# A retention layer's products in another order: rotary sums on VectorE, the second values' products behind the queries, the last head by halves of the tokens

## The chip, the cores and the metric

The kernel runs on one core of a Trainium2 chip. The metric is the device time of one launch in microseconds, the median of several runs. TensorE (PE) multiplies matrices and writes to PSUM; VectorE (DVE) and ScalarE (ACT) work on PSUM and SBUF; GpSimd (POOL) works on SBUF; SyncE (SP) issues the DMAs of this stage. Each engine takes its instructions in the order of its own queue, and semaphores order the engines among each other.

## The reference

Two layers of a diffusion backbone over 512 latent tokens with 256 context tokens and 1024 features, in fp32. The change touches layer 1, a bidirectional retention mixer with four heads (query and key width 256, value width 512), and the first steps of its feed-forward layer. Cut to what matters:

```python
q_x, k_x, v_x, g_x = split(h_x @ w_qkvg)          # 4 heads: 256, 256, 512, 512 each
q_x, k_x = rope_2d(q_x), rope_2d(k_x) * k_scale   # [x1 cos - x2 sin, x1 sin + x2 cos]
k_c, v_c = split(h_c @ w_qkvg[:, k and v])        # context: keys and values alone
state_f = retention_final_state(k_c, v_c); state_b = ...
o = retention_chunked(q_x, k_x, v_x, state_f) + flip(retention_chunked(flipped, state_b))
y = (o - mean) * rsqrt(var + EPS) * gn_gain       # per head, over its 512 values
x = x + mx[2] * ((silu(g_x) * y) @ w_o)
x = x + mx[5] * swiglu(modulate(rms_norm(x), mx[3], mx[4]))
```

## The kernel before, in words

Tiles have 128 partitions. Features lie on partitions, tokens along the free dimension, except in values, gates and the heads' outputs, where tokens lie on partitions. Every fp32 product is made of three matmuls on a high and a low part of each operand: `split` (line 163) casts a tile to its high part on ACT and subtracts it on VectorE for the low part (L164 and L165 in the profile). Weights come as 512 KB chunks of a stream in DRAM, through two raw buffers `wraw` (four others, `wx`, serve single chunks), each loaded by one DMA on SP's queue. Their two parts take one of four pairs of buffers in turn (`w_parts`, line 125); a pair is free when the product that read it has ended.

The retention layer multiplies the 512 tokens by the weights of one head at a time. In a head, query and key weights, and gate and value weights, are multiplied together as blocks: tokens are taken in halves (`HALVES`, line 31) and features in halves, and seven products of quarter size stand for eight. `quarter_of` names their operands: "11", "12" and "22" are quarters of the normed input, 1 to 4 are sums of quarters that `token_sums` (line 1125) makes once, in head 0. `product_q` and `product_v` (lines 1167, 1178) issue the matmuls of one such product: 24 of 256 columns for queries and keys, 24 of 512 for values and gates.

A head's loop body (line 1244) runs, in program order:

1. the first values' product into the two banks Z (`values_first`, issued in the head before, for head 0 ahead of the loop; line 1229);
2. the second values' product into banks X, and the context's values into the banks pj (lines 1252 to 1265);
3. keys into Y, X and pj (1271 to 1286), then the combined weights of the queries and five products (1289 to 1311);
4. the rotary of the queries (`rope_pair`, line 1191: two products on VectorE, L1196 and L1197, their sum or difference on GpSimd, L1198, and a split);
5. the combined weights of gates and values (1315 to 1328), the rotary of the keys, and products 2, 3 and "22" into the Z banks, which ACT copies out (L1333, L1336, L1340);
6. for each of six key tiles the scores, their decay factors and the sums over values (`scores`, `accumulate`, line 1347);
7. two more gate products into Z (1384 to 1397), the norm of the head's output, the gates, and the next head's first values;
8. 16 transposes of the gated output, the next head's context values, and eight output tiles added to the residual `xr` (`out_tile`, line 1442).

The last head makes its output tiles for the first half of the tokens and then for the second (line 1470). While the second half runs, the first half is normed for the feed-forward layer, whose first weights are split in between (`first_weights`, line 1462); its first products run on the first half too (`first_two`, line 1521), with the second half's norm (`second_half`) behind them.

The order on each engine is not written out by hand in this layer. The planner of the tile framework walks through the program, favours what comes earlier in it, and takes an instruction when, by its cost model, its operands and buffers are ready; `after` (line 91) adds an order between two instructions without a wait of its own. A tag's buffer count limits how far ahead a tile can be taken: 2 banks each for X, Y, Z and pj, 2 for `hn` and `sq`, 8 for `qk`.

Of the kernel before, what the change touches and what calls it, by code (L numbers as in the profile page):

```python
# [14 lines left out]
P = 128  # L15
# [34 lines left out]
def dit_kernel(ctx, tc, xT, cT, crow, small, consts, masks, tabs0, tabs1, jtab, adaQ, adaN, adaT, wst, out):  # L50
# [49 lines left out]
    def lnexp(*args, **kw):  # L100
        ins = nc.scalar.activation(*args, **kw)  # L101
        after(ins, [turn["pre"]])
        turn["lnexp"].append(ins)

# [1004 lines left out]
    def split_chunk(raw):  # L1109
        w = w_parts(qp)  # L1110
        split(raw, *w)
        return w

# [11 lines left out]
    def token_sums(hm, part, sh2, sums, behind=()):  # L1125
# [4 lines left out]
        for k in range(4):  # L1130
# [5 lines left out]
            for i, t in enumerate((t2, t1)):  # L1136
                split(t, *sums[2 * k + i])
# [8 lines left out]
    def latent_norm():  # L1146
        hm, b, y = [t_qk(F32) for _ in range(KT)], mods[1, 0], ssq[0]
        for k, t in enumerate(hm):
            nc.vector.scalar_tensor_tensor(t, xr[k], acol[1, 0, 0][:, k:k + 1], y, mult, mult)
# [4 lines left out]
        return hm  # L1154
# [36 lines left out]
    def rope_pair(o, cos1, sin1):  # L1191

        res = []
        for op, f0, f1 in ((sub, cos1, sin1), (add, sin1, cos1)):
# [3 lines left out]
            nc.gpsimd.tensor_tensor(a, a, b, op=op)  # L1198
# [5 lines left out]
    def strips(hd):  # L1204
# [6 lines left out]
        lnexp(dx[:, 512:896], jt[:, 128:512], AF.Exp, scale=lf)  # L1211
# [17 lines left out]
    def values_first(hd):  # L1229

        w = [split_chunk(chunk(chunk_base + 16 * hd + 4 + i)) for i in range(2)]
# [3 lines left out]
        return w, Y, ins  # L1235
# [6 lines left out]
    hm = latent_norm()  # L1242
    ahead_v = values_first(0)
    for hd in range(RH):
        bq = chunk_base + 16 * hd
        bv, bg = bq + 4, bq + 8


        b11, Yv, ins = ahead_v
        if hd == 0:  # L1250
            normed = context_norm([ins])
        b21 = [split_chunk(chunk(bv + i)) for i in (2, 3)]
        vt = [T(rp, 512, "res", 12) for _ in range(4)]
        for t in range(2):
            nc.scalar.copy(vt[t], Yv[t])
        Xv = [W4("X"), W4("X")]
        product_v(Xv, quarter_of("12"), b21, True)
        for t in range(2):
            nc.vector.tensor_tensor(vt[t], vt[t], Xv[t], op=add)
        if hd == 0:  # L1260
            cv = context_values(b11)
        product_v(cv, context_half(1), b21, False)
        vt += [T(rp, 512, "y0", 1), T(qp, 512, "vc", 1)]
        for t in range(2):
            nc.scalar.copy(vt[4 + t], cv[t])
# [483 lines left out]
```

## Time and profile before

| what | us |
|---|---|
| median of 3 runs | 1814.02 (1813.11 to 1815.79) |
| the profiled execution | 1812.0 |
| its span, first to last instruction | 1810.2 |
| TensorE busy in it | 1732.1 |
| VectorE busy | 1352.0 |
| retention layer, about | 905 to 1453 of the span |

The page of the profile gives shares over the whole span. Its views by window, by engine in order of time, and by wait are what the prediction works with. In a row of the timeline stand the start, the length, the engine, the line, the operation, the tiles written and read, the shape and the count; square brackets give the idle time before it and what ended it. In a row of windows stand the stretch, its length, and for each engine its busy time and number of instructions, then the granted TensorE clock (PEclk, 1.00 is full), the share of the DMA engines and GB/s.

### The profile page before, as it was taken

The page shows a single profiled execution, that of the slowest core. Times are in us where ns is not written, and L with a number is a line of the kernel's source. Part 1 is how long each engine was busy: PE and PEld are TensorE (multiplying, and loading weights), DVE is VectorE, ACT ScalarE, POOL GpSimd, SP SyncE. Part 2 cuts the span into 40 slices and gives each one's busy share as a digit, 9 for nine tenths or more (in the row PEclk, how much of TensorE's full clock was granted, in tenths as well). Part 3 has the DMA queues.
Part 4 walks back from the last instruction along what each step waited for, and adds up shares of the span by engine and source line. Part 5 has one row for each costly group of instructions (what it writes and reads, how often), then busy time and mean ns, then how long its engine had stood idle before and what let it go on. Part 6 is the DMA issues. An engine that isn't in the chain of part 4 may idle for free.

```text
span 1810.2 us, 27644 instructions
## 1 busy us (share of the span) xinstructions
PE 1732.1 (96%) x10876; PEld 1538.7 (85%) x10876; DVE 1352.0 (75%) x2327; ACT 835.0 (46%) x1461; POOL 163.9 (9%) x291
## 2 busy tenths in 40 slices
PE   6899999999999999999988999998999999999999
PEld 4777776799999999999877887887897889999998
DVE  6697786786688877777688758758757788777774
ACT  5476676363423333333454524524534454445432
POOL 0035334000000000000001001001001010000000
PEclk9999999999999999999988999999999999999999
DMA  9510002542244534343333424433433223233222
GB/s 338 224 36 24 24 2 82 182 141 86 90 134 126 162 118 143 118 147 117 95 107 128 156 89 130 146 94 129 146 113 97 93 71 98 90 117 117 84 92 82
DMA packets 59891, 206.69 MB, mean 114 GB/s; under 512 B 6640, under 2 KB 7024, under 8 KB 59504
## 3 DMA queue, kind: packets, MB, share of 16 engines
q1 hardware_dynamic: 52848, 179.75, 30.8%
q0 software_dynamic: 6912, 25.17, 4.6%
q8 instruction: 85, 1.39, 0.3%
q14 instruction: 46, 0.38, 0.1%
HBM read 202.80 MB, written 2.10 MB: 113 GB/s over the span
## 4 chain that ended last, share of the span: by engine, by line
PE 69%; DVE 16%; DMA 6%; ACT 4%; issue 3%; POOL 2%; SPq 0%; DVEq 0%; ACTq 0%; POOLq 0%
PE Y L834 12%; PE Z L834 6%; PE pj L148 6%; PE pj L149 6%; PE pj L147 6%; PE Z L1187 5%; PE X L834 3%; DVE wlo L165 3%; DMA wraw<-in_wst_dram 3%; PE pT L706 2%; DVE y L270 2%; DMA adaw<-in_adaT_dram 2%; PE pO L718 2%; PE S L683 2%; PE pj L1187 2%
## 5 line engine op out<-in xcount | busy, mean ns | idle before, releaser
L164 ACT CAST whi<-wraw 128x1024 fp32r<-128x1024 f32 x173 | 181.1, 1050 | 288.5 <-PE Z L149 73.6
L165 DVE TENSOR_TENSOR wlo<-wraw,whi 128x1024 fp32r<-128x1024 f32 x173 | 210.7, 1222 | 47.6 <-ACT whi L164 47.4
L834 PE MATMUL Y<-aq,whi 128*128 128x384 f32 x576 | 156.0, 335 | 0.6 <-ACT hn L974 0.5
L140 DVE TENSOR_TENSOR wlo<-wraw,whi 128x1024 fp32r<-128x1024 f32 x84 | 103.5, 1232 | 40.0 <-ACT whi L139 39.4
L252 DVE SCALAR_TENSOR_TENSOR res<-pj,mod,res 128x512 f32<-128x512 f32 (+1 forms) x112 | 81.5, 729 | 65.0 <-PE pj L149 63.9
L139 ACT CAST whi<-wraw 128x1024 fp32r<-128x1024 f32 x84 | 88.1, 1050 | 89.9 <-DMA wraw<-in_wst_dram 28.0
L834 PEld LDWEIGHTS Y<-aq,whi 128*128 128x128 f32 x576 | 104.8, 188 | 1.5 <-ACT hn L974 0.9
L834 PE MATMUL Y<-aq,wlo 128*128 128x384 f32 x288 | 96.6, 335 | 1.6 <-DVE wlo L165 1.6
L1187 PE MATMUL Z<-whi,sA 128*128 128x512 f32 x256 | 83.9, 400 | 6.6 <-ACT whi L164 3.6
L101 ACT ACTIVATE pr<-pr,stat,qs 128x513 f32<-128x513 f32 (+2 forms) x96 | 74.2, 776 | 30.7 <-DVE stat L690 29.9
L697 POOL TENSOR_SCALAR pr<-pr,stat 128x512 f32<-128x512 f32 (+2 forms) x96 | 67.1, 713 | 86.6 <-DVE stat L694 66.4
L270 DVE CUSTOM_DVE_ANT_0 y<-adaw,crow,small_sb 128x1024 bf16<-128x1024 f32 x48 | 61.4, 1278 | 14.5 <-DMA adaw<-in_adaT_dram 14.4
L1198 POOL TENSOR_TENSOR hn<-hn,sq 128x512 f32<-128x512 f32 x16 | 30.1, 1886 | 436.2 <-DVE sq L1197 432.6
L147 PE MATMUL pj<-ax,whi 128*128 128x512 f32 x176 | 68.7, 390 | 0.8 <-DVE res L252 0.8
L149 PE MATMUL pj<-ax,whi 128*128 128x512 f32 x176 | 68.7, 390 | 0.0
L148 PE MATMUL pj<-ax,wlo 128*128 128x512 f32 x176 | 68.5, 389 | 0.0
L706 PE MATMUL pT<-const_sb,pr 128*128 128x128 f32 x352 | 58.1, 284 | 9.8 <-POOL pr L697 7.6
L147 PE MATMUL pj<-act,whi 128*128 128x512 f32 x168 | 66.0, 393 | 0.0
L148 PE MATMUL pj<-act,wlo 128*128 128x512 f32 x168 | 65.9, 392 | 0.0
L1187 PEld LDWEIGHTS Z<-whi,sA 128*128 128x128 f32 x256 | 49.1, 192 | 19.6 <-ACT gate L1333 5.6
L149 PE MATMUL pj<-act,whi 128*128 128x512 f32 x168 | 65.5, 390 | 0.0
L706 PEld LDWEIGHTS pT<-const_sb,pr 128*128 128x128 f32 x352 | 38.8, 141 | 30.3 <-POOL pr L697 18.3
(504 smaller groups left out, 5382.1 us busy)
## 6 DMA issues: line engine op xcount, KB each, us to landing
wraw<-in_wst_dram SPq DMA_DIRECT2D x238, 512.0 KB, 3.6
adaw<-in_adaT_dram POOLq DMA_DIRECT2D x32, 512.0 KB, 3.9
wx<-in_wst_dram SPq DMA_DIRECT2D x24, 512.0 KB, 4.5
adan<-in_adaQ_dram SPq DMA_DIRECT2D x16, 512.0 KB, 8.2
adan<-in_adaN_dram SPq DMA_DIRECT2D x16, 512.0 KB, 8.7
crow<-in_adaT_dram POOLq DMA_DIRECT2D x16, 512.0 KB, 4.2
res<-in_xT_dram SPq DMA_DIRECT2D x16, 256.0 KB, 5.8
adaw<-in_adaT_dram SPq DMA_DIRECT2D x8, 512.0 KB, 4.1
```

The costliest lines, as they stand in the source:

```text
L139: nc.scalar.copy(hi, raw)
L140: nc.vector.tensor_tensor(lo, raw, hi, op=sub)
L147: nc.tensor.matmul(o, whi, xhi, start=first, stop=False)
L148: nc.tensor.matmul(o, wlo, xhi, start=False, stop=False)
L149: return nc.tensor.matmul(o, whi, xlo, start=False, stop=last)
L164: nc.scalar.copy(hi, t)
L165: return nc.vector.tensor_tensor(lo, t, hi, op=sub)
L252: return nc.vector.scalar_tensor_tensor(res[d], o, mods[l, s][:, part, d:d + 1], res[d], mult, add)
L270: after(nc.vector.tensor_tensor_reduce(junk, w, cr[:, s * 1024:(s + 1) * 1024], 1.0, sm_t[:, C_ADAB + l * 48 + j:C_ADAB + l * 48 + j + 1], ...
L706: nc.tensor.transpose(tp[:, a * P:(a + 1) * P], self.pr[(0, 2, 1, 3)[a]][:, ki * P:(ki + 1) * P], ident)
L834: nc.tensor.matmul(o, p, r, start=first and k + i == 0, stop=k == 3 and i == 2, skip_group_check=not first)
L1187: ins = nc.tensor.matmul(o, p, r, start=first and k + i == 0, stop=k == 3 and i == 2, skip_group_check=not first)
```

## The change

It touches the following.

- `rope_pair`: the sum of the two rotary products goes from GpSimd to VectorE.
- `latent_norm`: called for tiles 0 to 3 and 4 to 7, with the split of the first values' weights (`first_weights_v`) between them in program order, and the later tiles put behind that split on VectorE. The first values are copied out of Z in `values_first` itself.
- `other_values`: the second values' product and the context's values (step 2) become a function, called ahead of the keys in head 0 and behind the queries' rotary in heads 1 to 3. The context's keys `kc` go to a bank X instead of pj.
- `strips(0)`: its exponentials stand behind the token sums.
- The second half of the last gate product (tile 1) comes behind the gating of tiles 2 and 3, and in the last head also behind the transposes and casts of the second half of the tokens.
- The last head's output tiles run for the second half of the tokens first, in banks pj and Z, with the transposes and casts of the first half behind the fourth tile; then for the first half in X and Y. The norm of the feed-forward layer begins with the second half; an output tile's residual stands behind the norm four tiles back, and two of its four first weights behind the sixth norm. `first_two` begins with the second half.

```diff
-    def add_square(s, k, t, c=slice(None), eng=nc.vector, tmp=t_sq):
+    def add_square(s, k, t, c=slice(None), eng=nc.vector, tmp=t_sq, fresh=True):
...
-            if c.start in (None, 0):
+            if fresh:
...
-    def latent_norm():
-        hm, b, y = [t_qk(F32) for _ in range(KT)], mods[1, 0], ssq[0]
-        for k, t in enumerate(hm):
-            nc.vector.scalar_tensor_tensor(t, xr[k], acol[1, 0, 0][:, k:k + 1], y, mult, mult)
+    def latent_norm(ks, behind=()):
+        b, y = mods[1, 0], ssq[0]
+        for k in ks:
+            hm.append(t_qk(F32))
+            t = hm[k]
+            after(nc.vector.scalar_tensor_tensor(t, xr[k], acol[1, 0, 0][:, k:k + 1], y, mult, mult), behind)
...
-            nc.gpsimd.tensor_tensor(a, a, b, op=op)
+            nc.vector.tensor_tensor(a, a, b, op=op)
...
-    def strips(hd):
+    def strips(hd, behind=()):
...
-        lnexp(dx[:, 512:896], jt[:, 128:512], AF.Exp, scale=lf)
+        after(lnexp(dx[:, 512:896], jt[:, 128:512], AF.Exp, scale=lf), behind)
...
-    def values_first(hd):
-
-        w = [split_chunk(chunk(chunk_base + 16 * hd + 4 + i)) for i in range(2)]
+    def first_weights_v(hd):
+        return [split_chunk(chunk(chunk_base + 16 * hd + 4 + i)) for i in range(2)]
+
+    def values_first(w):
+
         Y = [W4("Z"), W4("Z")]
         ins = product_v(Y, quarter_of("11"), w, True, (0,))
         product_v(Y, quarter_of("11"), w, True, (1,))
-        return w, Y, ins
+        vt = [T(rp, 512, "res", 12) for _ in range(4)]
+        for t in range(2):
+            nc.scalar.copy(vt[t], Y[t])
+        return w, Y, vt, ins
...
-    hm = latent_norm()
-    ahead_v = values_first(0)
+    latent_norm(range(4))
+    b11 = first_weights_v(0)
+    latent_norm(range(4, KT), [last_split[0]])
+    b11, Yv, vt, ins = values_first(b11)
+    normed = context_norm([ins])
     for hd in range(RH):
...
+        def other_values():
+
+            b21 = [split_chunk(chunk(bv + i)) for i in (2, 3)]
+            Xv = [W4("X"), W4("X")]
+            product_v(Xv, quarter_of("12"), b21, True)
+            for t in range(2):
+                nc.vector.tensor_tensor(vt[t], vt[t], Xv[t], op=add)
+            c = cv if hd else context_values(b11)
+            product_v(c, context_half(1), b21, False)
+            vt.extend((T(rp, 512, "y0", 1), T(qp, 512, "vc", 1)))
+            for t in range(2):
+                nc.scalar.copy(vt[4 + t], c[t])
+
         if hd == 0:
...
+            other_values()
         k11, k21 = split_chunk(chunk(bq)), split_chunk(chunk(bq + 1))
         if hd == 0:
-            token_sums(hm, 0, T(qp, 64, "sh2", 1), h_sum, [normed])
-            dx, dcx = strips(0)
+            sums = token_sums(hm, 0, T(qp, 64, "sh2", 1), h_sum, [normed])
+            dx, dcx = strips(0, [sums])
         cos1, sin1 = rope_tables()
-        Y, X, kc = W4("Y"), W4("X"), pj()
+        Y, X, kc = W4("Y"), W4("X"), W4("X")
...
         qh = rope_pair(qt, cos1, sin1)
+        if hd:
+            other_values()
...
-        product_v(Zg, quarter_of(4), w22, False)
-        for t in range(2):
-            nc.vector.tensor_tensor(gate[t], gate[t], Zg[t], op=add)
+        product_v(Zg, quarter_of(4), w22, False, (0,))
...
+        gated(2)
+        gated(3)
+        if last:
+            transposes(1)
+            turned(HALVES[1])
+        product_v(Zg, quarter_of(4), w22, False, (1,))
+        for t in range(2):
+            nc.vector.tensor_tensor(gate[t], gate[t], Zg[t], op=add)
+            gated(t)
+        if not last:
+
+            b11, Yv, vt, ins = values_first(first_weights_v(hd + 1))
+            transposes(1)
+            transposes(0)
+            turned(slice(0, SX))
+            cv = context_values(b11)
...
-        for i, c in enumerate(HALVES):
+        for i, c in ((0, HALVES[1]), (1, HALVES[0])):
             for d in range(KT):
-                ins = out_tile(d, c)
-                add_square(0, d, xr[d], c, eng=(nc.vector, nc.gpsimd)[i])
+                ins = out_tile(d, c, "XY" if i else "jZ")
+                add_square(0, d, xr[d], c, eng=(nc.vector, nc.gpsimd)[i], fresh=i == 0)
+                if (i, d) == (0, 3):
+                    transposes(0)
+                    turned(HALVES[0])
                 if (i, d) in ((0, 5), (0, 7)):
                     first_weights(wx_parts)
-                if (i, d) in ((1, 3), (1, 5)):
-                    first_weights(hW_parts)
...
+                if (i, d) == (1, 1):
+                    rms(0, HALVES[1])
                 if i == 1 and d > 1:
-                    modulate(1, 0, 1, d - 2, xr, hx[d - 2], HALVES[0], hm[d - 2][:, HALVES[0]], [ins])
-        for k in (KT - 2, KT - 1):
-            modulate(1, 0, 1, k, xr, hx[k], HALVES[0], hm[k][:, HALVES[0]])
+                    done.append(second_norm(d - 2, HALVES[1], [ins]))
+                if i == 1 and d > 3:
+                    after(ins, done[d - 4:d - 3])
+        done += [second_norm(k, HALVES[1]) for k in (KT - 2, KT - 1)]
+        for _ in range(2):
+            first_weights(hW_parts, done[5:6])
...
-        for i, c in enumerate(HALVES):
+        for i in (1, 0):
+            c = HALVES[i]
             for f, (go, uo) in enumerate(banks):
-                project_pair(ahead[2 * f:2 * f + 2], half(i), (go[:, c], uo[:, c]), None if i + f else second_half, 5)
+                project_pair(ahead[2 * f:2 * f + 2], half(i), (go[:, c], uo[:, c]), second_half if i > f else None, 5)
```

New functions: `transposes(i)` issues the eight transposes of tiles 2i and 2i + 1 into banks X and Y; `turned(c)` scales and splits them for the tokens `c` (ACT and VectorE, L1434 and L1435 before); `gated(n)` is the silu of a gate tile and its product with the normed output; `second_norm` calls `modulate` for one tile and half.

More of the change, by code (lines that the diff above doesn't have):

```diff
@@ L1136, in token_sums @@
             for i, t in enumerate((t2, t1)):
-                split(t, *sums[2 * k + i])
+                last = split(t, *sums[2 * k + i])
+        return last
     def first_quarters(k, half):
@@ new lines, in dit_kernel @@
+        gated(2)
[7 more added lines that the diff above has]
+            gated(t)
+        if not last:
+            b11, Yv, vt, ins = values_first(first_weights_v(hd + 1))
[3 more added lines that the diff above has]
+            cv = context_values(b11)
@@ L1459, in dit_kernel, with first_weights @@
                       for n in ("hM", "hW", "hX"))
-        ahead, hx, hm = [], [], []
-        def first_weights(room):
+        ahead = []
+        def first_weights(room, behind=()):
             raw = w_raw()
-            ahead.append(room())
-            split(raw, *ahead[-1])
+            hi, lo = room()
+            ahead.append((hi, lo))
+            after(nc.scalar.copy(hi, raw), behind)
+            nc.vector.tensor_tensor(lo, raw, hi, op=sub)
         wx_parts = lambda: (T(qw, 1024, "wx", 4, F32R), T(qw, 1024, "wx", 4, F32R))
```

76 lines of the change are left out of this document (30 added, 46 removed).

## The prediction

> **What bounds the kernel now.** The page comes first: which engine is busy, and which engine the chain that ended last runs through.
>
> ```profile
> span 1810.2 us, 27644 instructions
> PE 1732.1 (96%) x10876; PEld 1538.7 (85%) x10876; DVE 1352.0 (75%) x2327; ACT 835.0 (46%) x1461; POOL 163.9 (9%) x291
> PE 69%; DVE 16%; DMA 6%; ACT 4%; issue 3%; POOL 2%; SPq 0%; DVEq 0%; ACTq 0%; POOLq 0%
> ```
>
> TensorE is the bound. The change removes no matmul, so it can only win time in which TensorE stands or runs slow. Such time is found by windows: the length of a stretch, less its matmuls times their undisturbed step. The first two rows give the steps, the next seven the stretches of the retention layer (905 to 1490 us) in which TensorE stands longest.
>
> ```profile
> core 0: us, PE busy (x) PEld busy (x) DVE busy (x) ACT busy (x) POOL busy (x), PEclk, DMA share, GB/s
> 1019.87:1030.75 10.88, 10.88 (x50) 9.01 (x48) 9.93 (x21) 5.56 (x8) 0.00 (x0) 1.00 0.51 205
> 1087.56:1099.08 11.52, 11.52 (x98) 11.47 (x96) 8.92 (x11) 6.15 (x11) 0.00 (x0) 1.00 0.68 216
> 907.97:929.45 21.48, 14.58 (x53) 10.88 (x52) 16.44 (x28) 10.54 (x19) 2.00 (x2) 0.76 0.51 171
> 951.73:988.50 36.77, 30.55 (x172) 26.39 (x170) 33.49 (x36) 16.98 (x26) 5.35 (x4) 0.86 0.35 112
> 1098.96:1122.39 23.43, 19.36 (x87) 15.22 (x86) 20.38 (x25) 10.33 (x16) 7.71 (x4) 0.93 0.24 78
> 1228.68:1253.05 24.37, 19.28 (x88) 15.17 (x87) 21.32 (x26) 10.54 (x16) 7.71 (x4) 0.93 0.26 83
> 1359.35:1382.37 23.02, 19.12 (x88) 15.21 (x86) 19.98 (x23) 10.04 (x16) 7.71 (x4) 0.93 0.19 53
> 1420.46:1452.97 32.51, 29.01 (x211) 27.72 (x209) 20.67 (x38) 15.62 (x28) 3.85 (x6) 0.90 0.35 117
> 1452.97:1485.13 32.16, 27.93 (x196) 26.15 (x195) 28.30 (x58) 19.78 (x35) 2.33 (x5) 0.89 0.32 100
> ```
>
> 48 matmuls of 512 columns in 10.88 us are 0.227 us each, 96 of 256 columns in 11.52 us are 0.12. By the code (missing records don't matter) and these steps:
>
> - **head 0, start** (907.97): 48 of 512, three small ones: 11.2 of 21.48 us, **10.3 lost**.
> - **head 0, queries to scores** (951.73): 121 of 256, 48 of 512: 25.4 of 36.77, **11.4 lost**.
> - **heads 1 to 3, the same place**: 25 of 256, 60 of 512: 16.6 us; lost **6.8, 7.8 and 6.4**, together 21.0.
> - **last head's output** (1420.46): 16 transposes (1.7 us), 192 of 256, two small: 25.0 of 32.51, **7.5 lost**.
> - **start of the feed-forward layer** (1452.97): 192 of 256, two small: 23.3 of 32.16, **8.9 lost**.
>
> Together 59.1 us. More than this the change cannot win.
>
> Why TensorE stops in heads 1 to 3 is read from the timelines of four engines in head 1:
>
> ```profile
> 1117.95 0.50 PE L1187 MATMUL Z<-whi,aq 128*128 128x512 f32 x1 [2.88 <-ACT gate L1336]
> 1119.56 1.05 PE L1187 MATMUL Z<-whi,aq 128*128 128x512 f32 x2
> 1120.41 0.63 PE L1187 MATMUL Z<-wlo,aq 128*128 128x512 f32 x1
> 1116.79 0.62 ACT L164 CAST qk<-hn 128x512 fp32r<-128x512 f32 x1 [4.79 <-POOL hn L1198]
> 1117.32 0.58 ACT L1336 COPY gate<-Z 128x512 f32<-128x512 f32 x1
> 1113.97 4.01 POOL L1198 TENSOR_TENSOR hn<-hn,sq 128x512 f32<-128x512 f32 x2 [7.04 <-DVE sq L1197]
> 1101.66 0.68 DVE L1197 TENSOR_TENSOR sq<-gate,rj 128x512 f32<-128x512 f32 x1
> 1102.87 1.78 DVE L1197 TENSOR_TENSOR sq<-gate,rj 128x512 f32<-128x512 f32 x1
> ```
>
> TensorE needs bank Z, which ACT must copy out (L1336). That copy stands in ACT's queue behind the cast of the rotated keys, and the cast waits 4.79 us for POOL's rotary add. The wait costs more than its length: from 1119.56 to 1120.41 two matmuls take 0.85 us, 0.43 each. That lasts some 9 matmuls, about 1.8 us more. The Trainium skill's page "TensorE: Matmul & The Clock Gate" (section "Why this matters for your kernels") puts the half clock behind gaps of about 3 us and more; here one of 2.88 us sufficed. By that rule a wait of 1 to 2 us left over in the changed kernel would cost its own length alone, as in the sum below.
>
> Head 0 is another case, VectorE's:
>
> ```profile
> 917.69 1.21 DVE L165 TENSOR_TENSOR wlo<-wraw,whi 128x1024 fp32r<-128x1024 f32 x1
> 917.16 0.80 PE L1187 MATMUL Z<-wlo,aq 128*128 128x512 f32 x1 [4.00 <-DVE wlo L165]
> 920.69 1.05 ACT L164 CAST whi<-wraw 128x1024 fp32r<-128x1024 f32 x1 [4.14 <-DMA wraw<-in_wst_dram]
> 976.34 1.22 PE L1187 MATMUL Z<-whi,sA 128*128 128x512 f32 x2 [3.55 <-ACT whi L164]
> 905.00:990.00 85.00, 71.77 (x393) 61.79 (x394) 76.46 (x114) 43.96 (x76) 10.37 (x8) 0.88 0.35 113
> ```
>
> The first values' products wait 4.00 us for the low part of their weights (L165), which VectorE makes only after the norm of all eight tiles; the next weights' DMA waits for the same buffer (4.14 us). But VectorE is busy 76.46 of 85 us: here it is the second bound.
>
> **The change part by part.** The profiled execution took 1812.0 us (span 1810.2); the median of the runs is 1814.02, so I add 2.0 at the end.
>
> *Rotary adds from POOL to VectorE* (L1198, four a head). Head 1's rows for what VectorE does beside them:
>
> ```profile
> L165 DVE TENSOR_TENSOR qk<-hn,qk 128x512 fp32r<-128x512 f32 x4 | 4.2, 1060 | 1.9 <-ACT qk L164 1.8
> L1197 DVE TENSOR_TENSOR sq<-gate,rj 128x512 f32<-128x512 f32 x4 | 3.8, 952 | 0.0
> ```
>
> Added: 16 VectorE adds of L1197's shape, 0.68 us undisturbed, 2.7 us a head. Gone: POOL's, the 4.01 us pair above included, and the stretching of VectorE's work beside them: 4 x (1.06 + 0.95 - 2 x 0.68) = 2.6 us a head. So VectorE's load stays level, and the path from product to cast shortens by 1 to 2 us at each add. POOL's queue issues no DMA here and loses nothing that others wait for.
>
> *X and context products behind the queries* (heads 1 to 3). 24 matmuls into X and 24 into pj, 48 x 0.227 = 10.9 us, go from before the keys to between the queries and product 2. They are cover: now 13.6 us of Z products (60 of 512) lie between the queries' end and the first score, then 24.5. What has to be done under them:
>
> ```profile
> 1040.00:1080.00 40.00, 40.00 (x194) 33.79 (x192) 21.41 (x24) 10.58 (x14) 0.00 (x0) 1.00 0.31 91
> 1065.17:1122.39 57.22, 53.15 (x325) 47.14 (x324) 42.22 (x47) 22.29 (x34) 7.71 (x4) 0.97 0.32 97
> L165 DVE TENSOR_TENSOR wlo<-wraw,whi 128x1024 fp32r<-128x1024 f32 x173 | 210.7, 1222 | 47.6 <-ACT whi L164 47.4
> L164 ACT CAST whi<-wraw 128x1024 fp32r<-128x1024 f32 x173 | 181.1, 1050 | 288.5 <-PE Z L149 73.6
> wraw<-in_wst_dram SPq DMA_DIRECT2D x238, 512.0 KB, 3.6
> ```
>
> From the end of the output tiles to the first score VectorE works 42.2 us; after, 42.2 + 2.7 - 2.6 = 42.3 us against 50.4 us of matmuls (57.22 less 6.8): it fits, at 84%. The order is tighter than the sum. w_parts (line 125) turns four pairs of buffers, and a pair is free when its product ends. With the second values' weights (two pairs) behind the queries, those of product 3 can be cut only when the context product ends: 1.05 (ACT) + 2 x 1.22 (VectorE) = 3.5 us, under the 5.4 us of product 2. Those of the last values follow under product 3, likewise. In SP's queue their two loads now stand behind the queries' and ahead of the gate's. The later one needs a buffer that is free when the last query weights are cut, some 17 us after the keys begin (keys 96 and queries 120 of 256: 25.9 us); it lands 3.6 us after issue, is cut by 23 and needed at 27. The gate's loads behind it make product 2's weights ready at about 31, needed at 36.8. Queued behind the rotated queries' casts on ACT are copies of X, pj and Z; the casts now wait for VectorE alone. The keys lose their cover of 10.9 us, but their weights can be cut during the output tiles, when VectorE is half idle (21.41 of 40 us). The bounds for the three heads are 21.0 (all stalls go) and, if VectorE comes late for both pairs, 6; I take **16** (5 us left), near the upper end because of the 84%.
>
> *Head 0*: its second values stay ahead of the keys. The split of the first weights goes between the norm of tiles 0 to 3 (all that the first product reads) and 4 to 7. The 4.00 us wait and the 4.14 us DMA wait mostly go. But the gain then stops at VectorE: it has 8.5 us of idleness in the 85, and the adds leave its load level. Bounds 2 and 8.5; I take **7**. The strips' six exponentials are put behind the token sums. ACT, busy 43.96 of 85 us, hides them; uncovered they are at most 6 x 0.91 = 5.5 us by the longest of them in a later head:
>
> ```profile
> 1145.62 0.91 ACT L101 ACTIVATE dcx<-rj,dcol,lg 128x640 f32<-128x640 f32 x1
> ```
>
> *Last head by halves*. Now: transposes wait for all gates, then the output for the casts of all four tiles.
>
> ```profile
> 1425.79 0.44 PE L147 MATMUL X<-qk,whi 128*128 128x256 f32 x1 [2.01 <-DVE qk L1435]
> 1454.55 0.38 PE L147 MATMUL X<-hx,wx 128*128 128x256 f32 x1 [1.43 <-ACT hx L241]
> 1454.12 1.22 DVE L165 TENSOR_TENSOR wlo<-wraw,whi 128x1024 fp32r<-128x1024 f32 x1 [0.25 <-ACT whi L164]
> 1455.26 0.48 DVE L242 SCALAR_TENSOR_TENSOR hx<-hm,mod,hx 128x256 fp32r<-128x256 f32 x1
> 1472.80 0.39 PE L147 MATMUL X<-hx,wx 128*128 128x256 f32 x1 [1.22 <-ACT hx L241]
> ```
>
> After: one half's eight transposes and casts lie under 12 matmuls of product 4 (2.7 us), the other half's under output tiles; a half has four casts on ACT and four rests on VectorE, which at 0.48 us each (1455.26's width) run side by side in some 2.4 us. Of 7.5 us lost I take **5.5** (bounds 2 and 7).
>
> *Start of the feed-forward layer*. VectorE cuts its weights (1454.12, and one more) between the norm's tiles while TensorE waits for them. After, norms come first by explicit order (an output tile's residual waits for the norm four tiles back), and the weights follow the sixth. But the two cuts (2 x 1.22 on VectorE, 2 x 1.05 on ACT) then meet the other half's norm, whose first tile is late already (1472.80). Of 8.9 I take **4.5** (bounds 0 and 8).
>
> Buffers taken elsewhere (kc in X, output tiles in pj and Z) cost nothing: their last readers end a product or more earlier.
>
> Sum: 16 + 7 + 5.5 + 4.5 = 33. 1812.0 - 33 = 1779.0; with 2.0, **1781**.
>
> **The rivals.**
>
> *VectorE becomes the bound.* For it: 76.46 of 85 us in head 0, 20.38 of 23.43 in head 1's stretch. The Trainium skill's "VectorE: DVE Perf Modes" (section "Rules for kernel authors") says to minimize the count of its operations, and this change adds 16. Against it: the 84%, and the 1.78 us rows. Then 4 us stay in each of heads 1 to 3 (9 won), head 0 wins 2, the rest 10: 21 us, **1793**.
>
> *The move isn't made.* The planner orders TensorE by what its model finds ready; it may run the X products ahead of a late query product. Then only POOL's wait goes: 10 of 16, the rest 17: 27 us, **1787**.
>
> *Slower: the ring of four weight pairs.* If VectorE is B us behind when the context product ends, TensorE stops B + 3.5 - 5.4 us before product 3 and about as long before the last values, each time with 1.8 us of half clock. At B = 8 that is 2 x (6.1 + 1.8) = 16 us a head, 48 in place of 21; with 17 won elsewhere, 10 us slower: **1824**. It decides above B = 6.5. For it: both rotary pairs (some 10 us) can stand in the queue then. Against: they do so only if the planner puts the keys' pair ahead of the weights.
>
> **How the numbers follow.** Forecast 0.65 (own range 1770 to 1790), VectorE bound 0.17, move not made 0.07, ring 0.06, and 0.05 that gains and new waits cancel within 0.2% (3.6 us, about what a measurement of this kernel tells from no change). Faster 0.89, same 0.05, slower 0.06. The range runs from 1768 (all upper bounds, 21 + 8.5 + 7 + 8 = 44.5 us, and 1.5 us of scatter) to 1803 (VectorE's case with the tail winning nothing) and leaves out the ring, the cancelling and little else.
>
> **What would show it.** Right: no wait of ACT for POOL in retention; X and pj products between queries and product 2; the three stretches short by 5 us or more each; first values without a wait for L165. Wrong: a wait for wlo or whi ahead of products 2, 3 or the last values, a half clock there, or new idleness ahead of the keys.

## The result, and the profile after

The changed kernel takes 1783.28 us (median of 4 runs, 1780.79 to 1784.84), the kernel before, beside it, 1814.71: a ratio of 0.9826, interval 0.9809 to 0.9843, so 31 us less. The forecast was 1781.0 in a range of 1768 to 1803. The profiled execution took 1781.98 us, its span 1780.2 (before 1812.0 and 1810.2).

First the page of the changed kernel: the span, the engines' busy times and the chain that ended last.

```profile
span 1780.2 us, 27618 instructions
PE 1721.0 (97%) x10876; PEld 1530.2 (86%) x10876; DVE 1346.5 (76%) x2347; ACT 834.1 (47%) x1465; POOL 134.4 (8%) x275
PE 72%; DVE 15%; DMA 5%; ACT 3%; issue 2%; POOL 2%; SPq 0%; DVEq 0%; ACTq 0%; POOLq 0%
```

The matmuls are as many as before. VectorE has 20 instructions more, 16 of them the rotary adds, yet is busy 5.5 us less (1352.0 before).

Next the stretches of the changed kernel, in windows that begin and end at the same work as those of before (the first two head 0, then heads 1 to 3 from the last keys to the first gate products, the last head's output, the start of the feed-forward layer, whose row runs on to 1460.00 where the same work ends at 1454.48, and last head 0 as a whole).

```profile
908.25:923.27 15.02, 12.39 (x54) 9.21 (x52) 14.80 (x25) 8.87 (x16) 2.48 (x2) 1.00 0.67 218
945.83:981.69 35.86, 28.80 (x171) 24.62 (x169) 32.36 (x39) 16.85 (x26) 0.00 (x0) 0.95 0.37 118
1080.81:1109.30 28.49, 27.98 (x136) 23.22 (x135) 26.15 (x33) 12.76 (x19) 0.00 (x0) 1.00 0.36 113
1205.89:1233.70 27.81, 27.81 (x136) 23.25 (x135) 26.83 (x34) 12.88 (x19) 0.00 (x0) 1.00 0.37 115
1330.29:1358.90 28.61, 27.94 (x136) 23.19 (x135) 26.21 (x34) 12.76 (x19) 0.00 (x0) 1.00 0.31 96
1395.41:1427.89 32.48, 29.91 (x224) 28.44 (x222) 25.95 (x52) 18.22 (x37) 4.16 (x8) 0.95 0.42 130
1427.89:1460.00 32.11, 30.09 (x243) 28.89 (x242) 30.08 (x61) 21.71 (x37) 1.66 (x2) 1.00 0.23 69
905.00:990.00 85.00, 75.17 (x425) 63.87 (x423) 79.42 (x123) 47.88 (x82) 3.99 (x4) 0.98 0.40 129
```

In heads 1 to 3 TensorE is busy all but 0.0 to 0.7 us of 28 at the full clock; before, it stood 4 to 5 us of 23 to 24 there at 0.93. In head 0 VectorE is now busy 79.42 of 85 us.

To see where the 30 us came from, every step of TensorE in both traces (start of one matmul to the start of the next) is set against its undisturbed step (0.227 us for 512 columns, 0.12 for 256); the excess is summed by place and called lost time below:

| lost, us | before | after | won |
|---|---|---|---|
| head 0 (895 to 1010) | 23.8 | 16.2 | 7.6 |
| heads 1 to 3 (1010 to 1395) | 22.9 | 7.8 | 15.1 |
| last head's output, start of the feed-forward layer (1395 to 1490) | 17.0 | 9.9 | 7.0 |
| all else | 65.5 | 65.9 | -0.5 |

The sum, 29.2 us, is the span's 30.0 but for 0.8. (The third row is 1.3 less than its two stretches won, since a later wait of 1.15 us, for a residual, falls inside its bounds now and its like, 0.82 us, fell behind them before.)

The list of TensorE's waits in the changed kernel (905 to 1490; total, number and longest) shows what is left; these are its first six rows of ten.

```profile
PE Z L1192 <- ACT whi L165: 3.3, 2, 1.7
PE Z L1192 <- DVE wlo L166: 2.6, 4, 0.9
PE pj L148 <- ACT qk L1449: 2.6, 2, 2.2
PE Y L1179 <- DVE wlo L166: 2.4, 2, 1.5
PE Y L1179 <- ACT whi L165: 2.2, 2, 1.8
PE X L1385 <- DVE wx L166: 2.1, 4, 0.6
```

The waits for gate copies of 2.88 us a head are gone, and the list of ACT's waits in retention has no row for POOL. What is left are mostly waits for weights in head 0, four of 0.6 us or less for VectorE in the heads (L1385), and one of 2.2 us at the last head's first output tile.

Waits are only half of it. All rows of the two lists add up to 33.6 us before and 18.6 after, 15.0 less, while the lost time of the first three places went from 63.7 to 33.9, 29.8 less. The other half is for the most part time in which matmuls ran slow. The stretch from 905 to 1490 us, before and after, shows it in its granted clock, 0.96 and 0.99:

```profile
905.00:1490.00 585.00, 550.23 (x2968) 475.14 (x2969) 435.76 (x614) 265.66 (x410) 39.77 (x30) 0.96 0.37 116
905.00:1490.00 585.00, 566.20 (x3173) 491.07 (x3172) 457.74 (x674) 277.70 (x433) 9.81 (x14) 0.99 0.38 120
```

### The profile page after: what moved, and what is told of

Its sections match the earlier page's. It is cut to its first block, busy times and chain, and to the rows that moved or that the text cites. A ratio compares the mean times of both kernels' runs of the same rounds, so it can differ in the third digit from the quotient of the medians.

```text
span 1780.2 us, 27618 instructions
## 1 busy us (share of the span) xinstructions
PE 1721.0 (97%) x10876; PEld 1530.2 (86%) x10876; DVE 1346.5 (76%) x2347; ACT 834.1 (47%) x1465; POOL 134.4 (8%) x275
## 4 chain that ended last, share of the span: by engine, by line
PE 72%; DVE 15%; DMA 5%; ACT 3%; issue 2%; POOL 2%; SPq 0%; DVEq 0%; ACTq 0%; POOLq 0%
PE Y L835 13%; PE Z L835 6%; PE pj L148 6%; PE pj L150 6%; PE pj L149 6%; DMA wraw<-in_wst_dram 3%; PE X L835 3%; PE Z L1192 3%; PE Y L1179 3%; DVE wlo L166 3%; PE pT L707 2%; PE S L684 2%; PE pO L719 2%; PE X L1179 1%; POOL pr L698 1%
## 5 line engine op out<-in xcount | busy, mean ns | idle before, releaser
L166 DVE TENSOR_TENSOR wlo<-wraw,whi 128x1024 fp32r<-128x1024 f32 x171 | 208.7, 1223 | 45.4 <-ACT whi L165 45.0
L707 PE MATMUL pT<-const_sb,pr 128*128 128x128 f32 x352 | 57.9, 284 | 10.8 <-POOL pr L698 8.5
L685 DVE CUSTOM_DVE_ANT_0 pr<-S,mask,qs 128x256 f32<-128x256 f32 (+1 forms) x96 | 53.2, 568 | 14.2 <-PE S L684 7.8
L835 PE MATMUL Y<-sA,whi 128*128 128x256 f32 x304 | 60.6, 282 | 0.0
```

What stands on the lines that cost most here:

```text
L166: return nc.vector.tensor_tensor(lo, t, hi, op=sub)
L707: nc.tensor.transpose(tp[:, a * P:(a + 1) * P], self.pr[(0, 2, 1, 3)[a]][:, ki * P:(ki + 1) * P], ident)
L835: nc.tensor.matmul(o, p, r, start=first and k + i == 0, stop=k == 3 and i == 2, skip_group_check=not first)
```

## The experiments

Each kernel is the changed one with one edit. It is compared with the kernel before, run on the same chip; the changed kernel's own ratio is 0.9826, and a difference of 0.001 in the ratio is 1.8 us. Medians differ by up to 3 us from one set of runs to the next (the kernel before: 1812.59 to 1815.67), so small differences are read from the lost time, of which each kernel has one trace:

| kernel | time, us | ratio (interval) | lost: head 0 | heads 1 to 3 | last head, feed-forward |
|---|---|---|---|---|---|
| changed | 1783.28 | 0.9826 (0.9809 to 0.9843) | 16.2 | 7.8 | 9.9 |
| pool_adds | 1797.01 | 0.9893 (0.9879 to 0.9908) | 20.5 | 16.0 | 9.6 |
| values_ahead | 1785.62 | 0.9826 (0.981 to 0.9843) | 17.7 | 10.4 | 9.1 |
| both_undone | 1798.8 | 0.9912 (0.9889 to 0.9935) | 20.4 | 20.1 | 9.5 |
| norm_whole | 1789.82 | 0.985 (0.9836 to 0.9865) | 20.8 | 6.9 | 12.0 |
| sums_twice | 1791.45 | 0.988 (0.9854 to 0.9905) | 21.4 | 7.2 | 9.7 |
| rope_lows_more | 1785.9 | 0.9848 (0.9826 to 0.9871) | 17.9 | 8.6 | 9.1 |
| pool_queries | 1791.38 | 0.988 (0.9862 to 0.9898) | 19.6 | 11.6 | 11.2 |
| pool_keys | 1795.62 | 0.9899 (0.9866 to 0.9932) | 17.4 | 10.8 | 9.0 |
| pool_beside | 1800.85 | 0.9917 (0.9895 to 0.9939) | 21.4 | 19.0 | 9.3 |
| whole_turn | 1785.89 | 0.9844 (0.9821 to 0.9867) | 16.7 | 6.7 | 9.8 |
| tail_order | 1782.49 | 0.9828 (0.9803 to 0.9854) | 17.9 | 7.7 | 7.0 |
| weights_early | 1791.98 | 0.9886 (0.9869 to 0.9903) | 18.6 | 6.9 | 18.6 |

Lost time scatters too. The last three kernels of the table have the changed kernel's code up to the last head, and yet lose 16.7 to 18.6 us in head 0 (16.2 in the changed kernel) and 6.7 to 7.7 in heads 1 to 3 (7.8); norm_whole and sums_twice differ from it only in head 0, and lose 12.0 and 9.7 at the end (9.9). So differences below some 2.4 us in head 0 or at the end, or below 1 us in heads 1 to 3, show nothing by themselves, and the changed kernel's 16.2 is the lowest of its kind.

### Which of the two edits wins in heads 1 to 3

The theory: the adds on VectorE end ACT's wait for POOL, and the moved products are the cover without which VectorE would be late. The rival: POOL was the whole cause. pool_adds undoes the first edit, values_ahead the second, both_undone both.

```diff
-            nc.vector.tensor_tensor(a, a, b, op=op)      # pool_adds
+            nc.gpsimd.tensor_tensor(a, a, b, op=op)
...
-        if hd == 0:                                      # values_ahead
-            other_values()
+        other_values()
...
-        if hd:
-            other_values()
```

> The changed kernel with the rotary adds back on GpSimd; everything else stays. Theory (both the adds and the moved products are needed, since each takes away part of the same waits): the 10.9 us of moved products cover the GpSimd adds in part, VectorE is stretched by about 2.6 us a head again; heads 1 to 3 lose 2 to 3 us each, head 0 about 1: some 1791 us. Rival (GpSimd is the whole cause): the stalls of 15 us come back, 1798. Rival (the moved products are the whole cause): within 1.5 us of the changed kernel's 1783.

> The changed kernel with the second values' and the context's products ahead of the keys in every head, as in the kernel before; the adds stay on VectorE. Theory: without the 10.9 us of cover the rotary and the gate weights are late again, though no longer for GpSimd: heads 1 to 3 lose 2 to 3 us each, some 1791 us. Rival (GpSimd is the whole cause): no change, 1783. Rival (the moved products are the whole cause): 15 us come back, 1798.

> The changed kernel with both undone: the rotary adds on GpSimd and the second values' products ahead of the keys. What is left of the gain is that of head 0's start and of the last head. From the traces heads 1 to 3 lost 22.8 us before and 7.8 after, so 15 us come back, and about 1 us in head 0: some 1799 us. The ACT waits for Z copies (2.9 us in each of heads 1 to 3) must be there again. If the two parts only add up, the loss here is the sum of the two runs that undo one; theory says more than the sum.

The rival is nearer in both. Without the move the ratio stays at 0.9826, and heads 1 to 3 lose 2.6 us more; without the adds it is 0.9893, 12 us more, and with both undone 0.9912. By lost time the 15.1 us of heads 1 to 3 divide so: 9.7 for the adds (20.1 of both_undone less 10.4), 2.6 for the move (10.4 less 7.8), and 2.8 for what else the change does there (22.9 of the kernel before less 20.1). The division depends on the order of undoing: taken from the changed kernel the adds are worth 8.2 (16.0 less 7.8), and then the move 4.1 (20.1 less 16.0). So both undone lose more than the two runs together, 12.3 us against 10.8, as that expectation had it. The 2.8 us lie between single traces, and no run takes them apart. On POOL the adds also cost 2 to 4 us in head 0 (20.5 against 16.2 to 18.6). The rows of both_undone show that the old wait returns (ACT in head 1, then TensorE; 4.79 and 2.88 us in the kernel before):

```profile
1113.03 0.62 ACT L165 CAST qk<-hn 128x512 fp32r<-128x512 f32 x1 [4.79 <-POOL hn L1203]
1113.55 0.58 ACT L1345 COPY gate<-Z 128x512 f32<-128x512 f32 x1
```

```profile
1114.18 0.50 PE L1192 MATMUL Z<-whi,aq 128*128 128x512 f32 x1 [2.84 <-ACT gate L1345]
```

In values_ahead the same TensorE wait is 0.75 us:

```profile
1108.96 0.50 PE L1192 MATMUL Z<-whi,aq 128*128 128x512 f32 x1 [0.75 <-ACT gate L1345]
```

### Which of the pairs, and what about POOL costs

```diff
-        qh = rope_pair(qt, cos1, sin1)
+        qh = rope_pair(qt, cos1, sin1, nc.gpsimd)        # pool_queries
...
-        kh = rope_pair(kt, cos1, sin1)
+        kh = rope_pair(kt, cos1, sin1, nc.gpsimd)        # pool_keys
```

> The changed kernel, with the rotary adds of the queries' pair alone back on POOL (8 adds in all), the keys' pair on VectorE. With both pairs on POOL the time was 12 to 13 us above the changed kernel. Theory: the pair whose casts hold up ACT's queue just ahead of the gate copies is the keys'; the queries' pair is early and has the products with X and the context behind it as cover: at most 4 us above the changed kernel's 1784, 1784 to 1788. Rival: both pairs cost alike, by their stretching of VectorE's work and by ACT's queue: about 6 us, 1790.

> The changed kernel, with the rotary adds of the keys' pair alone back on POOL (8 adds in all), the queries' pair on VectorE. Theory: this pair is the costly one, 8 to 12 us above the changed kernel's 1784, about 1794. Rival: both pairs cost alike: about 6 us, 1790.

The theory falls in one half: the queries' pair, for which it had at most 4 us, alone costs 10 by the ratio, and 7.2 in the lost time of head 0 and heads 1 to 3. The rival (6 us each) is nearer there, and also low. The keys' pair costs 13 us by the ratio, near the theory's 8 to 12, but its four runs reach from 1786.04 to 1799.27, and the profiled one is the lowest, with 3.3 us more lost than the changed kernel; how the costly ones differ is not seen. The two do not add up: together they cost 12.

An add on POOL could cost in two ways: by its length in the path to the cast, or by what it does to VectorE. Groups by line, VectorE's product (L1197, L1202) and low part, and POOL's add; first the kernel before, then the changed kernel (the add is L1203 there).

```profile
L1197 DVE TENSOR_TENSOR sq<-gate,rj 128x512 f32<-128x512 f32 x16 | 16.4, 1022 | 0.0
L165 DVE TENSOR_TENSOR qk<-hn,qk 128x512 fp32r<-128x512 f32 x16 | 17.6, 1101 | 6.0 <-ACT qk L164 5.4
L1198 POOL TENSOR_TENSOR hn<-hn,sq 128x512 f32<-128x512 f32 x16 | 30.1, 1886 | 436.2 <-DVE sq L1197 432.6 <-ACT qk L164 3.5
```

```profile
L1202 DVE TENSOR_TENSOR sq<-gate,rj 128x512 f32<-128x512 f32 x16 | 11.0, 686 | 0.0
L166 DVE TENSOR_TENSOR qk<-hn,qk 128x512 fp32r<-128x512 f32 x16 | 11.0, 687 | 0.0
L1203 DVE TENSOR_TENSOR hn<-hn,sq 128x512 f32<-128x512 f32 x16 | 11.0, 688 | 0.0
```

16 adds on POOL lengthened these two groups of VectorE (L1202 and L166 now) by 16.4 + 17.6 - 22.0 = 12.0 us. Done by VectorE itself they take 11.0 us (the last row), no more than it lost beside POOL. The Trainium skill's page "SBUF — State Buffer" (section "Who interferes with whom") says that a VectorE operation with two SBUF inputs contends with a GpSimd one that reads SBUF. The rows agree: 1.02 and 1.10 us in the mean beside POOL's adds, 0.69 without. pool_beside asks whether that alone is the cost: POOL multiplies as many elements beside each add, into a spare tile that nobody reads.

```diff
+            for n in range(4):
+                c = slice(n * P, (n + 1) * P)
+                nc.gpsimd.tensor_tensor(spare[0], o[0][:, c], f0[:, c], op=mult)
             nc.vector.tensor_tensor(a, a, b, op=op)
```

> The changed kernel, its rotary adds on VectorE, with POOL given as many elements to multiply beside each add (four 128x128 products of the same inputs into a spare tile that nobody reads): VectorE shares with POOL as in the kernel before, but no cast waits for POOL. Theory: POOL's adds cost by their latency, ahead of the casts in ACT's queue; VectorE's stretched operations (12.0 us over the 16 adds in the kernel before) fall into slack in heads 1 to 3 and cost only in head 0, a quarter of them: 1 to 4 us above the changed kernel's 1784, about 1786.5. Rival: the sharing itself is the cause: most of the 12 to 13 us that the adds on POOL cost come back, 1793 or more.

The rival's number came (1793 or more). But the dose was too large to settle the split. Head 1 of pool_beside, POOL, then the window of the stretch from the queries' rotary into product 2 (which begins at 1103.64), and TensorE's wait in that product:

```profile
1090.96 16.59 POOL L1207 TENSOR_TENSOR rj<-gate,rj 128x128 f32<-128x128 f32 x16 [104.80 <-DVE gate L1325]
```

```profile
1091.00:1108.00 17.00, 14.61 (x72) 12.06 (x71) 17.00 (x18) 5.26 (x9) 15.37 (x16) 0.99 0.30 93
```

```profile
1108.37 1.65 PE L1192 MATMUL Z<-whi,sA 128*128 128x512 f32 x3 [2.75 <-ACT whi L165]
```

POOL works 16.59 us without a pause (59.5 us in all, against 30.1 before), VectorE is busy 17.00 of 17.00 us, and the weights of the Z products come 2.75 us late. In heads 1 to 3 nothing on ACT waits for POOL (in head 0 one copy does, 3.39 us). So it is shown that POOL can stop TensorE here through VectorE alone, with no cast waiting for it; how the 12 us of pool_adds divide between that and the wait of the casts stays open. In pool_adds both are there: in heads 1 to 3 casts wait 32.1 us for POOL, and TensorE waits 8.2 us for weights (3.0 in the changed kernel) and only 1.3 us for a gate copy.

### How much room VectorE has

sums_twice makes the eight low parts of the token sums in head 0 twice; rope_lows_more makes each rotary low part in heads 1 to 3 three times.

```diff
+                if part == 0:                            # sums_twice
+                    last = nc.vector.tensor_tensor(sums[2 * k + i][1], t, sums[2 * k + i][0], op=sub)
...
+            for _ in range(more):                        # rope_lows_more
+                nc.vector.tensor_tensor(lo, a, hi, op=sub)
```

> The changed kernel, with the eight low-part subtractions of the token sums in head 0 made twice (the same result; 8 more 128x512 VectorE operations, about 0.6 us each, 4.8 us). Theory: what is left in head 0 (10.4 us lost between the queries and the scores) is VectorE's own load, 79.42 busy of 85 us, so the 4.8 us come through nearly whole: 4 to 5 us above the changed kernel's 1784, about 1788. Rival: head 0 waits for the latency of a chain that runs over ACT and the DMA, and VectorE has 5 us of slack there: below 1.5 us, 1784 to 1785.5.

> The changed kernel, with each low-part subtraction of the rotary pairs in heads 1 to 3 made three times (the same result; 8 more 128x512 VectorE operations a head, 24 in all, about 0.6 to 0.68 us each: 15 us of VectorE work). Theory: in heads 1 to 3 the queue of VectorE has room (42.3 of 50.4 us from the output tiles to the first score), so only a small part shows: at most 3 us, 1784 to 1787. Rival (VectorE is the bound there as in head 0, and the 2.6 us a head that were left are its): most of it shows, 10 to 15 us, 1794 to 1799.

By lost time both went as the theory had it. In head 0 4.8 us of work (eight steps of 0.6) cost 5.2 us (2.8 against the 18.6 of weights_early, the highest with the same code there); TensorE waits for the first keys' weights, whose cutting stands behind the sums:

```profile
954.99 0.58 PE L1181 MATMUL Y<-sA,whi 128*128 128x256 f32 x1 [7.14 <-ACT whi L165]
```

By the ratio it is 10 us, twice what the theory had; the profiled run is the lowest of the four, at 1788.52, and how the others differ is not seen. In heads 1 to 3 VectorE's busy time grew by 13.8 us (rope_lows_more; the group below; page 1360.3) and the lost time there by 0.8, within the scatter (the ratio has 4 us, in intervals that overlap). Waits for low parts did grow, to the second row's 4.3 us from 1.2, but the 1.8 us of waits at L1385 went.

```profile
L1207 DVE TENSOR_TENSOR qk<-hn,qk 128x512 fp32r<-128x512 f32 x24 | 16.5, 689 | 0.1
PE Z L1192 <- DVE wlo L166: 4.3, 3, 1.5
```

About as much VectorE time (15.1 us over the four heads, page 1361.6) cost 11.2 us there in pool_beside. The place alone does not explain that. Half of the extra low parts also stand ahead of product 2 (in head 1 four of them, from 1091.02 to 1096.45, with product 2 from 1098.27), where VectorE in the changed kernel is busy 13.87 us of 14:

```profile
1081.00:1095.00 14.00, 14.00 (x75) 12.07 (x75) 13.87 (x19) 4.13 (x8) 0.00 (x0) 1.00 0.36 108
```

So a full stretch still took 2.4 us a head (four steps of 0.6) for little. POOL's sharing lengthens nearly every operation in the 17 us of pool_beside above (0.69 to 0.95 us, 1.22 to 1.48), by some 3.5 us together, among them the sums of weights (L1340, L1341 of pool_beside) that ACT's casts wait for; three waits of TensorE of 2.75 to 2.80 us follow, with slow matmuls behind them (granted clock 0.55 from 1107 to 1113 us). That this larger dose, and its falling ahead of the casts, makes the difference is argued, not shown.

### The start of head 0

```diff
-    latent_norm(range(4))
+    latent_norm(range(KT))
     b11 = first_weights_v(0)
-    latent_norm(range(4, KT), [last_split[0]])
```

> The changed kernel with the norm of all eight latent tiles ahead of the first values' weights, as before. Theory: the first product waits about 4 us for the low part of its weights again and the second weights' DMA comes later; from the traces the start of head 0 lost 10.3 us before and 3.9 after, so 5 to 6 us come back: some 1789 us. Rival (VectorE's work sets the end of head 0 anyway, so an earlier start only makes TensorE wait later): at most 2 us come back, 1785.

The ratio says 4.4 us, the lost time in head 0 4.6 (2.2 against the 18.6 of weights_early): the theory holds, if a little high. The same wait at the first values' products, in norm_whole and then in the changed kernel (4.00 us before):

```profile
918.02 0.79 PE L1192 MATMUL Z<-wlo,aq 128*128 128x512 f32 x1 [3.34 <-DVE wlo L166]
```

```profile
911.89 0.50 PE L1192 MATMUL Z<-wlo,aq 128*128 128x512 f32 x1 [0.89 <-DVE wlo L166]
```

### The last head and the feed-forward layer

whole_turn turns the last head's output in one piece, behind the last gate product; tail_order puts the casts of the third and fourth output weights behind the first turned half; weights_early cuts the second pair of feed-forward weights among the output tiles, where the kernel before did.

```diff
+        if last:                                         # whole_turn
+            transposes(1)
+            transposes(0)
+            turned(slice(0, SX))
...
-        w += [next_w(qp) for _ in range(4)]
+        w += [next_w(qp) for _ in range(2)] + [next_w(qp, behind=[cast]) for _ in range(2)]   # tail_order
...
+                if (i, d) in ((1, 3), (1, 5)):           # weights_early
+                    first_weights(hW_parts)
...
-        for _ in range(2):
-            first_weights(hW_parts, done[5:6])
```

> The changed kernel, with the last head's sixteen transposes and their casts made whole, behind the last gate product, as in the kernel before; the output tiles still run by halves, the second half first. Theory (the prediction's last-head step, 5.5 us, of which the trace shows 2.7): without the halves the wait for all four casts comes back, 2 to 3 us above the changed kernel, about 1786.5. Rival: the halves themselves bring nothing, since the first output tile waits for a cast either way, and the 2.7 us come from the changed order of output tiles and buffers: within 1 us of 1784.

> The changed kernel, with the casts of the last two output weights put behind the last cast of the first turned half on ACT. In the changed kernel the first output tile waits 2.2 us for the cast of the turned half, which stands in ACT's queue behind a cast of output weights that waits 2.31 us for its DMA. Theory: that order is what is left of the last head's 4.8 us: 2 to 3 us below the changed kernel, about 1781.5, and the first output tile then starts without a wait for a turned half. Rival: the low parts of the turned half on VectorE, or the weights put back, are late next: within 1 us of 1784.

> The changed kernel, with the second pair of feed-forward weights cut where the kernel before cut it: among the output tiles (behind the fourth and the sixth of the second half) and not behind the sixth tile of the norm; all else stays. Theory: of the 5.6 us that the start of the feed-forward layer won, most come from keeping those two cuts behind the norm, since TensorE waits there for the norm's tiles: 3 to 5 us above the changed kernel's 1784, about 1788. Rival: they come from the order of the halves (the half whose tiles are ready first starts), and the place of the cuts is worth little: within 1 us of 1784.

whole_turn loses as much at the end as the changed kernel (9.8 and 9.9), as the rival had it: in the trace the halves bring nothing as they were ordered, and one wait stands for another. But the traced run is its fastest (1782.62; the others 1785.74 to 1786.92), and its ratio is 3 us higher, as the theory had it, in intervals that overlap. So whether the halves bring nothing or 3 us stays open. The first output tile of the changed kernel, of whole_turn (there it is the transposes that wait) and of tail_order:

```profile
1401.31 0.39 PE L148 MATMUL pj<-qk,whi 128*128 128x256 f32 x1 [2.21 <-ACT qk L1449]
```

```profile
1402.35 1.01 PE L1444 MATMUL X<-const_sb,gate 128*128 128x128 f32 x5 [2.73 <-DVE gate L1433]
```

```profile
1401.72 0.38 PE L148 MATMUL pj<-qk,whi 128*128 128x256 f32 x1 [0.56 <-ACT qk L1449]
```

Why the changed kernel waits 2.21 us is in its timeline of ACT: the first turned cast stands behind a cast of output weights that waits for its DMA.

```profile
1399.84 1.04 ACT L140 CAST whi<-wraw 128x1024 fp32r<-128x1024 f32 x1 [2.31 <-DMA wraw<-in_wst_dram]
1400.79 0.47 ACT L1449 ACTIVATE qk<-X,small_sb 128x256 fp32r<-128x256 f32 x1
```

tail_order removes that and loses 2.9 us less at the end, as expected. Its ratio (0.9828) does not show it: head 0 lost 1.7 us more in its profiled run, and the interval is 9 us wide. It is a better order there, not a kernel shown to be faster.

weights_early loses 8.7 us more at the end, twice what the theory had; its traced run is its slowest (1796.53; the others 1791.42 to 1792.09), but the medians too are 8.7 apart. The order of those two cuts thus carries more than the whole gain of the feed-forward layer's start (5.6): without it, the reversed halves and the new order of tiles leave the end no better than before (18.6 lost, and 17.0 before). Among its waits are two for the norm's tiles again:

```profile
1435.68 0.38 PE L148 MATMUL X<-hx,wx 128*128 128x256 f32 x1 [1.43 <-ACT hx L242]
1456.85 0.38 PE L148 MATMUL X<-hx,wx 128*128 128x256 f32 x1 [2.08 <-ACT hx L242]
```

## Why the prediction came out right, point by point

- **Heads 1 to 3: 16 forecast, 15.1 won.** The size came out right, in part by luck. Of the two causes the first, the wait for POOL, has the weight: the prediction gave it 10 of the 16 in the rival "the move isn't made", and the traces give it 9.7. The second, the 10.9 us of cover on which most of the working rests, was overrated: it was to bring the other 6, and values_ahead goes without it, with 2.6 us more lost in these heads and the same ratio. The other 2.8 us, which the prediction priced at nothing there and no run explains, made up for most of the difference. In the three stretches themselves (25 matmuls of 256 columns and now 108 of 512, 27.5 us by their steps) 2.4 us are left of the 21.0, less than the 5 forecast; the rest of the 7.8 lies between them.
- **VectorE's load stays level.** Forecast 2.7 us added and 2.6 saved a head; measured, over four heads, 11.0 added and 12.0 saved. The 84% was too mild a picture: it is an average over 57 us, and in the 14 us ahead of product 2 VectorE is busy 99%. Yet neither share says how much more it can take: with 2.4 us a head put into that stretch TensorE lost 0.8 us in all (rope_lows_more), with nearly every operation there lengthened 11.2 (pool_beside).
- **Head 0: 7 forecast, 7.6 won.** The cause was right: norm_whole gives back 4.6 us of it, and sums_twice fits that what is left is VectorE's. The 7.6 is the best of four traces with the same code there (5.2 to 7.6). The wait for the low part went from 4.00 to 0.89 us, not to nothing, and the weights' high part is waited for 1.74 us ahead of it.
- **Last head's output: 5.5 forecast, 2.7 won** (1395.41 to 1427.89 needs 27.7 us by its steps; 4.8 are lost, against 7.5). This is the term that was mis-sized. The step priced the casts that hang on the halves and not ACT's queue, in which a cast of weights, itself waiting for its DMA, stood ahead of them: 2.21 us, and slow matmuls behind it.
- **Start of the feed-forward layer: 4.5 forecast, 5.6 won** (3.3 lost up to 1454.48, against 8.9). The named cause, weights cut between the norm's tiles, is shown by weights_early; the feared collision with the other half's norm did not come (its first tile is waited for 0.97 us, 1.22 before).
- **The ring of four weight pairs** (1824) was not met: no product waits more than 0.7 us for its weights in heads 1 to 3.
- **A wait of 1 to 2 us costs its own length alone**, as the prediction took it from the Trainium skill's rule ("TensorE: Matmul & The Clock Gate", section "Why this matters for your kernels", gaps of about 3 us and more). The measurement decides against it: see the last section. The four terms, 33 us in the forecast, won 15.1 + 7.6 + 2.7 + 5.6 = 31.0; the sum is nearer than its terms, since 3.7 us too little in two of them stand against 1.7 too much in the others.

## What to carry to other kernels

Where one engine's queue holds a copy that frees TensorE's bank, ask what stands ahead of that copy and whom it waits for: moving 16 small adds to an engine that was already 75% busy won 12 us of the 31, and beside POOL's adds that engine had lost as much time as they cost it. How much more work an engine can take is not read off its busy share, neither over the stage (84%) nor in the few microseconds ahead of the product that needs it (99%): putting extra work there shows it. A rearrangement that is meant as cover should be tried without: here moving two products was worth 0 to 3 us as the kernel stands, and the order of two weight cuts 8.7.

## What the runs showed of the hardware

Waits of TensorE below 2 us are sometimes followed by a slow clock and sometimes not, at the same place and nearly the same length. The first keys' weights of head 0, in the changed kernel and then in weights_early:

```profile
947.95 0.38 PE L1179 MATMUL Y<-sA,whi 128*128 128x256 f32 x1 [1.84 <-ACT whi L165]
949.82 0.38 PE L1179 MATMUL Y<-sA,wlo 128*128 128x256 f32 x1 [1.48 <-DVE wlo L166]
950.04 0.40 PE L1179 MATMUL Y<-sA,whi 128*128 128x256 f32 x2
950.27 0.28 PE L1179 MATMUL Y<-sA,wlo 128*128 128x256 f32 x1
```

```profile
954.34 0.38 PE L1179 MATMUL Y<-sA,whi 128*128 128x256 f32 x1 [1.61 <-ACT whi L165]
956.25 0.39 PE L1179 MATMUL Y<-sA,wlo 128*128 128x256 f32 x1 [1.53 <-DVE wlo L166]
957.06 0.63 PE L1179 MATMUL Y<-sA,whi 128*128 128x256 f32 x2
957.48 0.41 PE L1179 MATMUL Y<-sA,wlo 128*128 128x256 f32 x1
```

After waits of 1.84 and 1.48 us two matmuls take 0.23 us (950.04 to 950.27); after 1.61 and 1.53 us they take 0.42 (957.06 to 957.48).

The first values' products show the same with one code and nearly equal waits: 1.74 and 0.89 us in the changed kernel, 1.76 and 0.89 in tail_order. The 16 us around them, in this order, have a granted clock of 1.00 and 0.89:

```profile
909.00:925.00 16.00, 13.85 (x57) 10.56 (x58) 15.78 (x26) 9.56 (x17) 2.48 (x2) 1.00 0.69 229
909.00:925.00 16.00, 13.35 (x51) 10.55 (x51) 15.34 (x25) 9.62 (x17) 2.48 (x2) 0.89 0.67 223
```

So part of the scatter of the lost time is the clock's. That it also explains the scatter of medians from run to run is argued, not shown.
